# Strassen operand sums made by the producer and spilled, and one plain pair per stage

## The chip, the cores and the metric

The kernel runs on one core of one Trainium2 chip. The metric is the time of one execution in microseconds (us) on the device. Engines are named as in the profile: PE (TensorE), DVE (VectorE), ACT (ScalarE), POOL (GpSimd) and SP (SyncE); SP computes nothing and issues most transfers, and 16 DMA engines carry them.

## The reference

One decoder layer in float32, for 512 tokens of 2048 features. What matters here is the sequence of matrix products after the attention part:

```
merged = sigmoid(g_a) * (y_a @ w_up_a) + sigmoid(g_b) * (y_b @ w_up_b)
x  = x + merged @ w_o                                   # 2048 x 2048
h  = rmsnorm(x, ffn_norm_g)
hid = h @ w_ffn_in                                      # 2048 x 11264
x  = x + (silu(gate) * up) @ w_ffn_out                  # 5632 x 2048
x  = x + sigmoid(rmsnorm(x, ple_norm_g) @ w_ple_gate) * (p @ w_ple)
```

## The kernel before, in words

Activations are kept transposed: features on the 128 partitions, the 512 tokens along the row. A *unit* is 256 features of the contraction, so its operand is four blocks of 128 x 256 (two feature halves by two token halves), called b0 to b3. Every number is split into a high part (`hi`, made on ACT) and a low rest (`lo`, made on DVE), and a product takes high x high, high x low and low x high.

A *pair* (class `Pair`) computes 256 output features from all units of a stage (eight in most). A unit enters a pair in one of two kinds. Kind `P`, plain: eight block products, in twelve matmuls 512 wide (`mm3`, lines 286 to 298). Kind `S`, Strassen: seven products of sums of blocks. Its operand has seven blocks: the four plain ones, and three sums of them; the fourth plain block is overwritten by another sum (b3 − b1, held as `v`) once the plain form is no longer used. A pair of `S` alone issues 512- and 256-wide matmuls on line 694 (`doubled=7`); a pair with both kinds uses `mm3` 256 wide (the gate: `doubled=5`). `mix`, `mix_doubled` and `rest` recombine the products on DVE and ACT (lines 720, 750, 753, 799).

Weights come in *doubles* (two units). For `S` five blocks are landed from memory by SP (lines 341, 343), two more are added onto them by an accumulating transfer from POOL (line 363), and two sums are made on DVE (line 375); for `P` four blocks are landed (line 339). ACT splits the high part (line 359), DVE the low (line 356). Four landing buffers and three slots of split weights turn round.

The stages follow each other: the up-projections write the merged rows ("mix"), w_o makes x1, FFN-in (44 pairs) makes the inner rows ("hid", 22 units), FFN-out runs in three passes over 8, 8 and 6 units (`PASSES`), the last making x2, and the gate product closes. The rows of one stage are the units of the next. They are stored to memory (`spill`) and loaded again (`load`, line 518) as a *form* (`late_form`, `plain_first`): the first load is split to the plain blocks; a second load of the same row is gained and summed on DVE (line 527) into the three sums and `v`, which are then split. Until both are there a unit enters as `P`: the tuples `HALF`, `FFN_UNTIL`, `PLAIN_UNTIL`, `GATE_UNTIL` say for how many pairs each unit is plain.

What is loaded when is decided while the program is written out. `tick` runs after a part of each pair (eight times a pair of eight units): it fetches a first load for one of the next three forms, steps the first form, fetches one second load, and runs what was put off with `after`. A form whose plain use is over and whose second load has not been fetched is *urgent*: while there is one, no first load is fetched. Working blocks lie in the arena `wholes`, operands in `parts`, which has room for eight Strassen forms. Outputs of pairs, squares of rows and the like go to two 'out' buffers that turn round (`wide`). `Norm.add` squares a row (ACT) and adds it up (DVE).

Of the kernel before, what the change touches and what calls it, by code (L numbers as in the profile page):

```python
# [19 lines left out]
P = 128  # L20
# [35 lines left out]

PRODUCTS = (1, 2), (5, 4), (4, 3), (3, 6), (0, 5), (2, 0), (6, 1)

# [12 lines left out]
def hybrid_layer(  # L71
# [137 lines left out]
    def tick():  # L209
# [235 lines left out]
    class Form(Staged):  # L445


        def __init__(self, kind, steps, sizes, ready, src=None, far=False):
# [4 lines left out]
            self.second, self.due_second, self.forced, self.stage = None, 0, False, -1  # L453

        def fetch(self):
# [76 lines left out]
    def plain_first(form, raw, gain):  # L532
# [25 lines left out]
        if form.used:  # L558
            tt(b[:, 2:0:-1], b[:, 4:2:-1], twice(b[:, 1]))
            tt(b[:, 3], b[:, 2], b[:, 0], ALU.add)  # L560
            yield
            split_into(x[:, 3:7, 0], x[:, 3:7, 1], b[:, 1:5])
            give(w)
            return
        v = take(256, "old")
        tt(v.f(), b[:, 3], b[:, 1])
        tt(b[:, 2], b[:, 4], b[:, 1])
        tt(b[:, 3], b[:, 2], b[:, 0], ALU.add)
        yield
        split_into(x[:, 4:7, 0], x[:, 4:7, 1], b[:, 2:5])  # L570
        give(w)
        yield
        while not form.used:
# [4 lines left out]
    def all_first(form, raw):  # L578
# [4 lines left out]
        split_into(x[:, 0:4, 0], x[:, 0:4, 1], b)  # L583
        tt(t[:, 2], b[:, 3], b[:, 2])
        tt(v.f(), b[:, 3], b[:, 1])
        tt(t[:, 0], t[:, 2], b[:, 1])
        tt(t[:, 1], t[:, 0], b[:, 0], ALU.add)
        give(raw)
# [9 lines left out]

    def late_form(src, ready=always, gain=None, far=False):
# [10 lines left out]
        return Form("S", steps, [(parts, 2 * PLACE, "place"), (wholes, 1024, "low")], ready,  # L610
                    src, far)

# [336 lines left out]
    class Norm:  # L949
# [4 lines left out]
        def add(self, raw):  # L954
# [8 lines left out]
            if self.done == KU:  # L963
                self.chain = Staged(self.steps())
                self.chain.go_on()

        def steps(self):
# [309 lines left out]
    def plan_rest():  # L1277
# [5 lines left out]
        for j in range(KU):  # L1283
            plan(w_o[j], now("S" * KU, HALF, j))
        for m in range(KH):
# [16 lines left out]
    for n, ((w, i), pr) in enumerate(zip(order, made())):  # L1302
# [25 lines left out]
        else:  # L1328
# [9 lines left out]
             for j in range(KU)}  # L1338
    there = set()

    def spilled_form(kind, n, j, gain=None, **how):
        return (late_form if kind == "S" else plain_form)(
            lambda size=1024: load(spill[n, j], size), lambda: (n, j) in there, gain, far=True,
            **how)

# [7 lines left out]
    for j in range(KU):  # L1353
        for b in "ba":
# [13 lines left out]
            else:  # L1368
                nc.vector.tensor_tensor(out=g, in0=g, in1=part[j].f(), op=ALU.add)
# [13 lines left out]
    for j in range(KU):  # L1383
        h = load(xT[j])
        if j == 1:
            build(fs)
        pr = pair(ms, last=j == KU - 1, j=j, until=HALF, doubled=7)
        pr.onto(h.f())
        nc.sync.dma_start(out=spill["x1", j], in_=h.f())
        there.add(("x1", j))  # L1390
        norm2.add(h)
        give(h)
# [6 lines left out]
    for kinds in PASSES:  # L1399
        hs.append([spilled_form(k, "hid", u)  # L1400
                   for u, k in enumerate(kinds, sum(map(len, hs)))])
    def hidden(m, o):
        g, row2 = o[:, :T], norm2.row()
# [23 lines left out]
    for c, units in enumerate(hs):  # L1427
# [3 lines left out]
        for j in range(KU):  # L1431
# [14 lines left out]
            there.add(("x2", j))  # L1446
            norm3.add(h)
            give(h)
# [128 lines left out]
```

## Time and profile before

| | |
|---|---|
| median of 3 runs | 2655.95 us (2654.94 to 2663.76) |
| profiled execution, span | 2655.1 us |
| PE, DVE, ACT, POOL busy | 99%, 85%, 53%, 17% of the span |
| moved by DMA | 561.46 MB, mean 211 GB/s; 51.38 MB written to memory |
| granted PE clock | 0.999 |

The profiled execution's span is the time from its first to its last instruction, and the only time that the profile gives for it. A busy PE is not a PE at its best: matmuls overlap, so what a stage costs is read from the time between the starts of its pairs. "DMA share" in a window is the mean busy share of the 16 DMA engines; PE, DVE and the others stand with their busy time and, in brackets, their instructions.

### The profile page before, as it was taken

How to read it: one execution, taken by the hardware profiler on the slowest of the kernel's cores; microseconds unless marked ns; L12 is line 12 of the kernel's file. 1: busy time of each engine (PE TensorE's matmuls, PEld its weight loads, DVE VectorE, ACT ScalarE, POOL GpSimd, SP SyncE). 2: the span in 40 equal slices, each digit the busy share in tenths (PEclk: the TensorE clock that was granted, in tenths of full speed). 3: DMA queues.
4: the chain of work that ended last, by engine and by line, in shares of the span. 5: the costliest groups of instructions: out<-in, count | busy, mean ns of one | idle time of the engine just before them, and what ended most of it. 6: DMA issues, size and time to landing. Idle time of an engine off the chain costs nothing.

```text
span 2655.1 us, 42310 instructions
## 1 busy us (share of the span) xinstructions
PE 2633.3 (99%) x15188; PEld 2299.5 (87%) x15188; DVE 2254.2 (85%) x3856; ACT 1410.3 (53%) x2245; POOL 449.9 (17%) x556
## 2 busy tenths in 40 slices
PE   8999999999999999999999999999999999999998
PEld 6888888888998888888888888888888888889888
DVE  8687878787887558999888888888889989989897
ACT  7756565655554334566444444444445545455643
POOL 0122223232220001101111111111110211211010
PEclk9999999999999999999999999999999999999999
DMA  7676777777775668978888888888787989988784
GB/s 228 161 197 168 192 174 186 177 187 184 181 187 190 230 209 269 265 236 212 229 215 215 199 201 210 197 205 200 196 214 218 259 221 276 230 233 262 241 274 132
DMA packets 288130, 561.46 MB, mean 211 GB/s; under 512 B 26288, under 2 KB 133552, under 8 KB 287920
## 3 DMA queue, kind: packets, MB, share of 16 engines
q1 hardware_dynamic: 226576, 442.87, 50.9%
q0 software_dynamic: 61344, 115.89, 27.5%
q8 instruction: 119, 1.95, 0.3%
q14 instruction: 91, 0.75, 0.1%
HBM read 507.28 MB, written 51.38 MB: 210 GB/s over the span
## 4 chain that ended last, share of the span: by engine, by line
PE 94%; DVE 3%; ACT 1%; DMA 1%; issue 1%; SPq 0%; POOL 0%; ACTq 0%; DVEq 0%
PE ps L694 56%; PE ps L298 9%; PE ps L297 9%; PE ps L296 9%; PE small L694 6%; DVE wlo L356 1%; PE small L1158 1%; PE small L1106 1%; PE small L1032 1%; DVE wholes L527 0%; DVE parts L287 0%; DVE wholes L375 0%; ACT whi L359 0%; PE small L1217 0%; PE small L298 0%
## 5 line engine op out<-in xcount | busy, mean ns | idle before, releaser
L694 PE MATMUL ps<-parts,whi 128*128 128x512 f32 x4390 | 1470.1, 398 | 1.7 <-DVE out L799 1.3
L359 ACT ACTIVATE whi<-wholes 128x512 fp32r<-128x512 f32 (+2 forms) x934 | 874.3, 948 | 757.8 <-DVE wholes L375 295.3
L356 DVE TENSOR_TENSOR wlo<-wholes,whi 128x512 fp32r<-128x512 f32 (+2 forms) x934 | 982.5, 1087 | 79.5 <-ACT whi L359 78.7
L694 PEld LDWEIGHTS ps<-parts,wlo 128*128 128x128 f32 x4390 | 824.2, 188 | 187.3 <-issue 1.9
L694 PE MATMUL ps<-parts,wlo 128*128 128x256 f32 x4390 | 868.2, 279 | 0.9 <-DVE wlo L356 0.9
L694 PEld LDWEIGHTS ps<-parts,whi 128*128 128x128 f32 x4390 | 706.8, 189 | 10.3 <-issue 3.1
L296 PE MATMUL ps<-parts,whi 128*128 128x256 f32 (+1 forms) x1612 | 534.0, 333 | 6.9 <-ACT parts L286 4.9
L298 PE MATMUL ps<-parts,wlo 128*128 128x256 f32 (+1 forms) x1622 | 539.3, 333 | 0.7 <-DVE wlo L356 0.6
L297 PE MATMUL ps<-parts,whi 128*128 128x256 f32 (+1 forms) x1622 | 539.3, 333 | 0.7 <-DVE parts L287 0.5
L375 DVE TENSOR_TENSOR wholes<-wholes 128x256 f32<-128x256 f32 x820 | 347.0, 423 | 17.7 <-DVE wlo L356 2.8
L753 DVE TENSOR_TENSOR out<-out,ps 128x256 f32<-128x256 f32 x525 | 217.4, 417 | 158.0 <-ACT out L750 157.8
L297 PEld LDWEIGHTS ps<-parts,whi 128*128 128x128 f32 x1622 | 306.3, 189 | 37.6 <-DVE parts L287 2.6
L296 PEld LDWEIGHTS ps<-parts,whi 128*128 128x128 f32 x1612 | 304.0, 189 | 38.4 <-ACT parts L286 5.9
L298 PEld LDWEIGHTS ps<-parts,wlo 128*128 128x128 f32 x1622 | 306.7, 189 | 30.8 <-DVE wlo L356 2.0
L363 POOL DMA_DIRECT2D wholes<-w_ffn_in x169 | 147.1, 870 | 702.5 <-DMA wholes<-w_ffn_in 205.8
L363 POOL DMA_DIRECT2D wholes<-w_in x132 | 117.1, 888 | 527.5 <-DVE wholes L375 111.3
L694 PE MATMUL small<-parts,whi 128*128 128x512 f32 x480 | 190.2, 397 | 0.0
L287 DVE TENSOR_TENSOR parts<-wholes,parts 128x1024 fp32r<-128x1024 f32 (+3 forms) x139 | 124.5, 906 | 17.7 <-ACT parts L286 17.7
L750 ACT ACTIVATE out<-ps 128x256 f32<-128x256 f32 x279 | 105.1, 385 | 61.4 <-PE ps L694 56.9
L286 ACT ACTIVATE parts<-wholes 128x1024 fp32r<-128x1024 f32 (+3 forms) x139 | 107.9, 797 | 54.4 <-DVE wholes L527 37.7
L363 POOL DMA_DIRECT2D wholes<-w_ffn_out x64 | 55.7, 871 | 358.1 <-DVE out L753 76.7
L1405 ACT ACTIVATE out<-out 128x512 f32<-128x512 f32 x44 | 27.8, 633 | 152.2 <-DVE out L1404 152.2
(132 smaller groups left out, 1825.3 us busy)
## 6 DMA issues: line engine op xcount, KB each, us to landing
wholes<-w_ffn_in SPq DMA_DIRECT2D x169, 384.0 KB, 5.6
wholes<-w_in SPq DMA_DIRECT2D x132, 384.0 KB, 5.0
wholes<-w_ffn_in SPq DMA_DIRECT2D x169, 256.0 KB, 4.8
wholes<-w_ffn_in POOLq DMA_DIRECT2D x169, 256.0 KB, 5.4
wholes<-w_in SPq DMA_DIRECT2D x132, 256.0 KB, 4.0
wholes<-w_in POOLq DMA_DIRECT2D x132, 256.0 KB, 5.1
wholes<-w_ffn_out SPq DMA_DIRECT2D x64, 384.0 KB, 6.0
wholes<-x SPq DMA_DIRECT2D x46, 512.0 KB, 6.0
```

Of the source, the lines that this page charges most:

```text
L286: return (nc.scalar.activation(hi, src, AF.Copy), nc.vector.tensor_tensor(out=lo, in0=src, in1=hi.bitcast(F32), op=ALU.subtract))
L287: nc.vector.tensor_tensor(out=lo, in0=src, in1=hi.bitcast(F32), op=ALU.subtract))
L296: nc.tensor.matmul(ps, sh, mh, start=start, stop=False)
L297: nc.tensor.matmul(ps, sh, ml, start=False, stop=False)
L298: return nc.tensor.matmul(ps, sl, mh, start=False, stop=stop)
L356: in_turn(nc.vector.tensor_tensor(out=self.lo[:, blocks], in0=r, in1=h.bitcast(F32), op=ALU.subtract))
L359: in_turn(nc.scalar.activation(h, r, AF.Copy))
L363: nc.gpsimd.dma_start(out=raw[:, 3:5], in_=self.src[:, 1:3], accum_op=ALU.add)
L375: in_turn(nc.vector.tensor_tensor(out=o, in0=x, in1=y, op=ALU.add))
L694: m = nc.tensor.matmul(out, l, r, start=first and k == 0, stop=last and k == 1)
L750: in_turn(nc.scalar.activation(out, x, AF.Copy, scale=scale))
L753: in_turn(nc.vector.tensor_tensor(out=out, in0=x, in1=y, op=op))
```

## The change

The sums of a row are made where the row is made, and stored beside it: for the merged rows (`leave`), x1 and those x2 rows that the gate uses as Strassen units (`gained_sums`, after the gain), and the FFN inner rows (`hidden`, from the two halves of a unit that lie in the two 'out' buffers). The second load of a form now fetches the three sums and `v` as two blocks, and only splits them. It waits until the sums have been issued (`ready_second`). Every unit is plain in the first pair of its stage only. The products are renumbered to the order in which the sums lie.

```diff
-HALF = 1, 1, 1, 1, 2, 2, 2, 2
-PLAIN_UNTIL = HALF, HALF, (2, 2, 2, 2, 1, 1)
+O_UNTIL = (1,) * 8
+PLAIN_UNTIL = (1,) * 8, (1,) * 8, (1,) * 6
-GATE_UNTIL = 1, 1, 2, 2, 2, 2, 1, 1
+GATE_UNTIL = (1,) * 8
-FFN_UNTIL = 1, 1, 2, 2, 2, 2, 2, 2
+FFN_UNTIL = (1,) * 8
...
-PRODUCTS = (1, 2), (5, 4), (4, 3), (3, 6), (0, 5), (2, 0), (6, 1)
+PRODUCTS = (1, 2), (5, 5), (4, 3), (3, 4), (0, 6), (2, 0), (6, 1)
...
-            if (f.used or not any(b.stage == f.stage and b.ready() and not b.there
-                                  for b in builds)) and fits([(wholes, 5 * 256, "old")]):
+            if f.ready_second() and (
+                    f.used or not any(b.stage == f.stage and b.ready() and not b.there
+                                      for b in builds)) and fits(
+                        [(wholes, 768, "old"), (wholes, 256, "old")]):
                 f.fetch_second()
...
-            self.second, self.due_second = self.src(5 * 256), clock[0] + WAIT
+            self.second, self.due_second = self.sums(), clock[0] + WAIT
...
-        w = form.second
-        b = cut(w.f())
-        if gain:
-            gained(w.f(0, 1024), w.f(0, 1024), *gain)
-            yield
-        tt(b[:, 4], b[:, 3], b[:, 2])
...
-        v = take(256, "old")
-        tt(v.f(), b[:, 3], b[:, 1])
-        tt(b[:, 2], b[:, 4], b[:, 1])
-        tt(b[:, 3], b[:, 2], b[:, 0], ALU.add)
-        yield
-        split_into(x[:, 4:7, 0], x[:, 4:7, 1], b[:, 2:5])
-        give(w)
-        yield
+        t, v = form.second
+        split_into(x[:, 4:7, 0], x[:, 4:7, 1], cut(t.f()))
+        give(t)
         while not form.used:
             yield
         split_into(x[:, 3, 0], x[:, 3, 1], v.f())
...
+    def second_blocks(n, j):
+        blocks = take(768, "old"), take(256, "old")
+        d = sum_spill[n, j]
+        nc.sync.dma_start(out=blocks[0].f(), in_=d[:, 256:1024])
+        nc.sync.dma_start(out=blocks[1].f(), in_=d[:, 0:256])
+        return blocks
...
+    def sums_into(o, x):
+        tt(o[:, 0:2], twice(x[:, 3]), x[:, 1:3])
+        tt(o[:, 2], o[:, 1], x[:, 1])
+        tt(o[:, 3], o[:, 2], x[:, 0], ALU.add)
+
+    def spill_sums(n, j, o, x):
+        sums_into(cut(o), cut(x))
+        nc.sync.dma_start(out=sum_spill[n, j], in_=o)
+        there.add((n, j, "sums"))
+
+    def gained_sums(n, j, h, gi, sq):
+        t = wide()
+        gained(t, h.f(), gi, j)
+        return lambda: spill_sums(n, j, sq, t)
...
-                give(part.pop(j))
-                after(1, lambda j=j, s=s: store("mix", j, s))
+                def leave(j=j, s=s, other=other):
+                    spill_sums("mix", j, other.f(), s.f())
+                    give(other)
+                    store("mix", j, s)
+
+                after(1, leave)
...
-        norm2.add(h)
+        after(1, gained_sums("x1", j, h, g_ffn, norm2.add(h)))
...
+        halves.append(cut(o))
         if m % 2 == 1:
             there.add(("hid", m // 2))
+            (x, y), u = halves, m // 2
+            halves.clear()
+            if ("hid", u) in sum_spill:
+                tt(y[:, 2], y[:, 1], x[:, 1])
+                tt(y[:, 3], y[:, 1], y[:, 0])
+                tt(x[:, 2], y[:, 3], x[:, 1])
+                tt(x[:, 3], x[:, 2], x[:, 0], ALU.add)
+                for i, b in enumerate((y, x)):
+                    nc.sync.dma_start(out=cut(sum_spill["hid", u])[:, 2 * i : 2 * i + 2],
+                                      in_=b[:, 2:4])
+                there.add(("hid", u, "sums"))
...
-            norm3.add(h)
+            sq = norm3.add(h)
+            if GATE[j] == "S":
+                after(1, gained_sums("x2", j, h, g_ple, sq))
```

More of the change, by code (lines that the diff above doesn't have):

```diff
@@ L445, in hybrid_layer, with __init__ @@
     class Form(Staged):
-        def __init__(self, kind, steps, sizes, ready, src=None, far=False):
+        def __init__(self, kind, steps, sizes, ready, src=None, far=False, sums=None,
+                     ready_second=None):
             super().__init__(steps(self))
@@ L453, in __init__ @@
             self.second, self.due_second, self.forced, self.stage = None, 0, False, -1
+            self.sums, self.ready_second = sums, ready_second
         def fetch(self):
@@ L597, in all_first, with late_form @@
         give(v)
-    def late_form(src, ready=always, gain=None, far=False):
+    def late_form(src, ready=always, gain=None, far=False, sums=None, ready_second=None):
         def steps(form):
@@ L610, in late_form @@
         return Form("S", steps, [(parts, 2 * PLACE, "place"), (wholes, 1024, "low")], ready,
-                    src, far)
+                    src, far, sums, ready_second)
     def plain_form(src, ready=always, gain=None, raw=1024, how="low", far=False):
@@ L965, in add @@
                 self.chain.go_on()
+            return sq
         def steps(self):
@@ L1283, in plan_rest @@
         for j in range(KU):
-            plan(w_o[j], now("S" * KU, HALF, j))
+            plan(w_o[j], now("S" * KU, O_UNTIL, j))
         for m in range(KH):
@@ L1368, in hybrid_layer @@
             else:
-                nc.vector.tensor_tensor(out=g, in0=g, in1=part[j].f(), op=ALU.add)
-                give(part.pop(j))
-                after(1, lambda j=j, s=s: store("mix", j, s))
+                other = part.pop(j)
+                nc.vector.tensor_tensor(out=g, in0=g, in1=other.f(), op=ALU.add)
+                def leave(j=j, s=s, other=other):
[3 more added lines that the diff above has]
+                after(1, leave)
         if not j:
@@ L1386, in hybrid_layer @@
             build(fs)
-        pr = pair(ms, last=j == KU - 1, j=j, until=HALF, doubled=7)
+        pr = pair(ms, last=j == KU - 1, j=j, until=O_UNTIL, doubled=7)
         pr.onto(h.f())
@@ L1401, in hybrid_layer @@
                    for u, k in enumerate(kinds, sum(map(len, hs)))])
+    halves = []
     def hidden(m, o):
```

22 lines of the change are left out of this document (9 added, 13 removed).

## The prediction

> **What bounds the kernel now.** I read the page first (busy shares, chain, DMA queues), then the PE timeline for the places where the operations change form (line 694 is a Strassen pair, lines 296 to 298 a plain or mixed one), then windows cut at those places, then the waits and the chain in the windows that ran long.
>
> ```profile
> span 2655.1 us, 42310 instructions
> PE 2633.3 (99%) x15188; PEld 2299.5 (87%) x15188; DVE 2254.2 (85%) x3856; ACT 1410.3 (53%) x2245; POOL 449.9 (17%) x556
> q1 hardware_dynamic: 226576, 442.87, 50.9%
> q0 software_dynamic: 61344, 115.89, 27.5%
> PE 94%; DVE 3%; ACT 1%; DMA 1%; issue 1%; SPq 0%; POOL 0%; ACTq 0%; DVEq 0%
> ```
>
> TensorE is never off for long, so time is gained by issuing fewer columns or by closing the few holes. The sum is made against this execution's 2655.1 us, 0.03% under the median of 2655.95 us. A difference under about 0.3%, 8 us, can hardly be told from no change here.
>
> ```profile
> core 0: us, PE busy (x) PEld busy (x) DVE busy (x) ACT busy (x) POOL busy (x), PEclk, DMA share, GB/s
> 839.20:1005.10 165.90, 165.90 (x734) 137.41 (x733) 90.72 (x98) 58.28 (x65) 0.88 (x1) 1.00 0.64 216
> 1005.10:1068.80 63.70, 62.55 (x342) 53.95 (x341) 55.96 (x94) 33.52 (x44) 7.91 (x9) 1.00 0.92 276
> 1068.80:1146.90 78.10, 78.10 (x449) 68.15 (x448) 73.53 (x129) 38.83 (x52) 14.08 (x16) 1.00 0.93 253
> 1146.90:1166.70 19.80, 19.80 (x114) 17.21 (x113) 19.67 (x35) 13.17 (x20) 0.89 (x1) 1.00 0.68 208
> 1166.70:1231.70 65.00, 64.85 (x341) 55.38 (x340) 61.79 (x114) 47.08 (x70) 8.19 (x9) 1.00 0.82 237
> 1270.80:1973.70 702.90, 702.90 (x4033) 613.29 (x4032) 622.77 (x1117) 337.17 (x468) 126.14 (x145) 1.00 0.82 206
> 2032.50:2094.90 62.40, 62.40 (x343) 54.24 (x342) 61.85 (x103) 34.38 (x45) 8.77 (x10) 1.00 0.96 276
> 2192.70:2257.20 64.50, 63.12 (x343) 53.78 (x342) 61.42 (x100) 34.87 (x45) 9.64 (x11) 1.00 0.97 274
> 2355.10:2387.20 32.10, 32.10 (x146) 26.68 (x145) 29.24 (x49) 14.41 (x20) 4.38 (x5) 1.00 0.86 248
> 2387.20:2465.00 77.80, 77.80 (x546) 73.09 (x546) 71.92 (x111) 40.74 (x53) 6.97 (x8) 1.00 0.85 260
> 2481.10:2527.40 46.30, 45.49 (x219) 37.65 (x218) 41.14 (x71) 31.29 (x47) 4.72 (x5) 1.00 0.84 257
> 2527.40:2588.90 61.50, 61.50 (x365) 54.30 (x364) 55.35 (x89) 27.42 (x38) 7.92 (x9) 1.00 0.89 272
> ```
>
> The rows are, in order: the plain up-projections from the second on; w_o pairs 0 to 2; 3 to 6; 7; FFN-in pairs 0 to 2; 36 steady FFN-in pairs; the first three pairs of FFN-out pass 0; of pass 1; the first two of pass 2; pass 2's pairs 2 to 6; gate pairs 0 and 1; gate pairs 2 to 4. The reader should see three things. TensorE is full everywhere. VectorE is at 95 to 99% of the windows in which operands are made (61.79 of 65.00, 61.85 of 62.40, 61.42 of 64.50). And the DMA engines are at 0.92 to 0.97 there.
>
> **The price of a unit on TensorE.** The plain window holds 14 half-pairs of four units and five small products of the same twelve matmuls: 61 units, 2.72 us each. A Strassen unit costs 702.90 / 36 / 8 = 2.44 us in a pure pair, (77.80 / 5 − 2 x 2.72) / 4 = 2.53 in pass 2's mixed pair, and (61.50 / 3 − 2 x 2.72) / 6 = 2.51 in the gate's.
>
> **What the plain pairs become.** The second pair of each stage turns Strassen: 4 units in w_o, 6 in FFN-in, 4 in each of three passes, 4 in the gate, 26 together; pure pairs also lift the units that were mixed from 2.53 to 2.44. A plain pair takes 21.76, a pure one 19.53.
> - w_o: now 63.70, with 62.3 by the prices (21.76 + 4 x 2.53 + 4 x 2.72 + 19.53). After 21.76 + 2 x 19.53 = 60.8: gain 2.9 if the 1.4 us of holes go too.
> - FFN-in: now 65.0, by the prices 62.7; the other 2.3, the norm's small products and what they wait for, I keep. 60.8 + 2.3 = 63.1: gain 1.9.
> - Pass 0: 62.4 to 60.8, gain 1.6. Pass 1: 64.5 to 60.8, gain 3.7, of it 2.2 holes.
> - Pass 2: 32.1 to 16.3 + 15.6 = 31.9, gain 0.2, since its mixed pair is little cheaper than a plain one.
> - Gate: 4 x (2.72 − 2.51) = 0.8.
>
> Sum 11.1 us, 7.5 without the holes of w_o and pass 1.
>
> **Do the holes go?** They are VectorE's.
>
> ```profile
> PE ps L694 <- DVE out L799: 1.2, 2, 0.8
> PE ps L694 <- DVE wlo L356: 0.9, 1, 0.9
> by line: DVE wlo L356 22.6%; DVE wholes L527 22.5%; PE ps L694 22.1%; issue 12.2%; DVE parts L287 8.4%; DVE wholes L375 7.3%; DVE out L720 3.6%; PE ps L298 0.5%; PE ps L297 0.5%; PE ps L296 0.5%
> ```
>
> The first is w_o's start, the second pass 1's, the third the chain from 2225 to 2250 us: line 527, the consumer's sums, stands in front of the weight splits. Where those sums lie today:
>
> ```profile
> 1005.10:1068.80 63.70, 9.00 (x23) 1.00 0.92 276
> 1166.70:1231.70 65.00, 12.46 (x30) 1.00 0.82 237
> 2032.50:2094.90 62.40, 12.08 (x28) 1.00 0.96 276
> 2192.70:2257.20 64.50, 12.03 (x28) 1.00 0.97 274
> 2387.20:2465.00 77.80, 3.03 (x8) 1.00 0.85 260
> 2481.10:2527.40 46.30, 6.14 (x16) 1.00 0.84 257
> ```
>
> (VectorE's time on line 527 alone.) The change takes it away there and puts it where the rows are made.
>
> **What VectorE pays instead.**
>
> ```profile
> L356 DVE TENSOR_TENSOR wlo<-wholes,whi 128x1280 fp32r<-128x1280 f32 x8 | 11.9, 1487 | 0.1
> L375 DVE TENSOR_TENSOR wholes<-wholes 128x256 f32<-128x256 f32 x16 | 6.7, 421 | 0.1
> L356 DVE TENSOR_TENSOR wlo<-wholes,whi 128x512 fp32r<-128x512 f32 x8 | 5.5, 686 | 0.0
> L356 DVE TENSOR_TENSOR wlo<-wholes,whi 128x1024 fp32r<-128x1024 f32 x4 | 4.9, 1221 | 0.0
> ```
>
> A double of Strassen weights costs (11.9 + 6.7 + 5.5) / 8 = 3.0 us, a plain one 1.2: +1.8. A spilled sum is one 512-wide and two 256-wide instructions, 0.69 + 0.84 = 1.5 us; a unit of FFN inner rows four 256-wide, 1.7 per two pairs. A pure pair's recombination is 12 x 0.42 + 0.69 = 5.7 against a mixed one's 4 x 0.42 + 2 x 0.69 = 3.1: +2.6.
> - Up-projections: 1.5 per pair of half-pairs, and VectorE is at 90.72 of 165.90. Nothing; TensorE covers it. Steady FFN-in: 622.77 / 36 = 17.3 per pair plus 0.85, of 19.53. Nothing, with 1.4 us to spare.
> - w_o and the start of FFN-in as one stretch (1005.1 to 1231.7, 226.6 us): VectorE has 210.95. Out: 9.00 + 12.46. In: nine sums (the last merged row, eight x1) 13.8, one inner unit 1.7, five doubles 9.0, two recombinations 5.2. That is 219.2 of an ideal 221.8; in w_o pairs 3 to 7 alone it is 93.2 + 7.7 = 100.9 of 97.9, over by 3.0, of which weights split ahead and operands split late absorb part.
> - Pass 0: 61.85 − 12.1 + 3.6 + 2.6 = 56.0 of 60.8; pass 1 much the same. VectorE stops being tight. Pass 2's pairs 2 to 6: 71.92 − 3.0 + 5 x 1.5 = 76.5 of 77.8; between nothing and 2, I take 0.5. Gate: 41.1 − 6.1 + 3.6, easier.
>
> ScalarE does the gains it did before, at another time, and is at 53%. GpSimd gets 13 more accumulating transfers, at 17%: nothing.
>
> **What the DMA engines pay.** From the queue rows: 1.60 us of all 16 engines for 512 KB (442.87 MB in 50.9% of the span), 0.83 us for 128 KB accumulated (115.89 MB in 27.5%). A converted unit lands five blocks instead of four and accumulates two: 0.20 + 0.83 = 1.03. Sums are 42 stores of 512 KB, 22 MB; loads of them replace loads as large.
>
> ```profile
> 2094.90:2114.40 19.50, 19.50 (x114) 17.01 (x113) 17.45 (x32) 7.67 (x11) 5.83 (x7) 1.00 1.02 250
> ```
>
> - w_o and FFN-in's start: 58.6 + 72.6 + 13.5 + 53.3 = 198.0 now. Plus ten units 10.3, nine stores 14.4, one inner unit 1.6: 224.3, against 221.8 of TensorE. The fullest pair I found, above, has 1.02, so this stretch cannot reach its ideal: 2.5 back, and with VectorE's 3.0 in the same pairs I take 3.0, between 0 (transfers moved forward into the up-projections, share 0.64) and 7 (the two added, and late operands).
> - Pass 0: 59.9 + 4.1 = 64.0 of 60.8. The last FFN-in pair before it can take some, as the sums lie ready long before; I take 0.5 back, 0 to 3. Pass 1: 62.6 + 4.1 = 66.7 of 60.8; I take 1.5, 0 to 5.
> - Pass 2 and gate: 27.6 + 4.1 of 31.9; 38.9 + 4.1 of 45.5. Nothing.
>
> **Waits and queues.** SyncE waits in order, and a store of sums waits for VectorE:
>
> ```profile
> SPq L341 <- DVE wlo L356: 1331.1, 379, 10.1
> SPq L1389 <- DVE wholes L375: 26.5, 6, 5.4
> ```
>
> Behind a store stand the weight loads of line 341, which already wait 3.5 us each for the same engine to free a landing. The x1 store waits 4.4 us today; the second store behind it adds about the sums' 1.5, inside the weights' lead. SyncE issues 62 more stores and 42 more loads: nothing. The 'out' buffers of a pair are held one tick, an inner row's one pair longer, and are next written in the last quarter of the pair after: nothing. Were that cover gone, it would be one store's landing, some 5 us, per pair.
>
> **Sum.** 11.1 − 3.0 − 0.5 − 1.5 − 0.5 = 5.6: 2649.5, rounded to 2650.
>
> **Rivals.**
> (a) The DMA engines do not bind; their share only tells that work is queued. Then only VectorE's half microseconds are given back: 10 us gained, 2645. For it: pass 0 ran with 0.96 and no hole. Against it: pass 1 with 0.97 had holes, but VectorE's. [...] The trace does not decide it: its starts never moved more than 276.
> (b) The operands come late: second pairs now need all eight sums after one pair, not two, and each of five starts loses about 2 us. The gain is spent: 2655. For it: pass 1 still summed on line 527 in its third pair, from 2235.9 us on (first row below). Against it: VectorE, which delayed them, has less to do.
>
> ```profile
> 2240.73 0.42 DVE wholes L527
> wholes<-x SPq DMA_DIRECT2D x46, 512.0 KB, 6.0
> L286 ACT ACTIVATE parts<-wholes 128x1024 fp32r<-128x1024 f32 x8 | 8.3, 1052 | 2.6 <-DVE wholes L527 2.6
> L287 DVE TENSOR_TENSOR parts<-wholes,parts 128x1024 fp32r<-128x1024 f32 x9 | 11.0, 1220 | 0.0
> ```
>
> (c) Slower: used forms go first. While a used form has not loaded its second part, no first part is fetched, and from the third tick of a first pair all forms become used two at a time. If the last first half is not fetched in the first two ticks, TensorE meets a load and its split: landing 6.0 us, split 1.05 and 1.22 (rows above), about 8 us. It decides if two or more starts are hit: three give 24 − 5.6, some 2669, two 2660, centre 2664. Against it: seven of eight rows exist a pair earlier.
>
> **Chances.** Forecast 0.45 (2647 to 2654), (a) 0.25 (2643 to 2648), (b) 0.15 (2653 to 2660), (c) 0.15 (2659 to 2670). Range 2643 to 2663, leaving out the upper half of (c) and a little of (a). Faster than 2648: (a) and the forecast's lower edge, 0.30. Slower than 2664: 0.13 from (c) and the edge of (b). Within: 0.57.
>
> **What would show it.** Second pairs of w_o, FFN-in and passes 0 and 1 without lines 296 to 298 and near 19.5 us; line 527 gone; no wait of PE on line 799 or 356 at pass 1's start; w_o pairs 3 to 6 above 78.1 us with VectorE near full and DMA share near 1; written bytes up by 22 MB. A PE wait of several us on lines 286 or 287 in a first pair is (c); w_o pairs 3 to 6 still at 78.1 with a share over 1.0 is (a). I am wrong most if the list that places transfers orders them otherwise than the ticks do.

## The result, and the profile after

The changed kernel took 2671.41 us in the median of 4 runs (2667.22 to 2673.83), the kernel before 2655.9 beside it: 1.0054 times as long, interval 1.004 to 1.0068. That is 0.54% slower, where 2650 had been predicted and 2663 was the range's end. The profiled execution of the changed kernel was its fastest, 2667.22 us with a span of 2665.4, so its trace shows 10.3 us of the loss and not the whole of it. The page, busy times and bytes:

```profile
PE 2633.5 (99%) x15175; PEld 2299.6 (86%) x15175; DVE 2279.7 (86%) x3929; ACT 1418.5 (53%) x2277; POOL 455.7 (17%) x569
HBM read 512.39 MB, written 73.40 MB: 220 GB/s over the span
```

Written bytes rose by the predicted 22.0 MB, and TensorE's busy time is that of before: what its plain units saved came back as time. The stages, in the windows of the prediction (in order: w_o pairs 0 to 2; 3 to 6; FFN-in 0 to 2; three pairs of pass 0; of pass 1; pass 2 pairs 0 and 1; 2 to 6; gate pairs 0 and 1):

```profile
core 0: us, PE busy (x) PEld busy (x) DVE busy (x) ACT busy (x) POOL busy (x), PEclk, DMA share, GB/s
1004.00:1067.70 63.70, 61.23 (x322) 51.81 (x321) 56.73 (x94) 36.00 (x52) 8.78 (x10) 1.00 0.99 302
1067.70:1146.30 78.60, 78.38 (x450) 68.07 (x449) 76.74 (x139) 42.73 (x61) 14.99 (x17) 1.00 0.99 282
1166.00:1232.30 66.30, 64.58 (x338) 54.80 (x337) 63.61 (x113) 42.75 (x65) 10.81 (x12) 0.97 0.93 273
2033.20:2094.60 61.40, 60.86 (x321) 51.94 (x320) 57.71 (x93) 34.84 (x52) 11.34 (x13) 1.00 1.01 297
2192.40:2253.00 60.60, 60.60 (x321) 51.97 (x321) 55.34 (x88) 34.54 (x51) 11.37 (x13) 1.00 1.04 304
2352.50:2387.90 35.40, 33.39 (x183) 29.39 (x182) 30.10 (x47) 19.86 (x28) 3.52 (x4) 0.95 0.91 254
2387.90:2472.40 84.50, 80.88 (x548) 74.96 (x546) 72.40 (x110) 40.58 (x53) 7.84 (x9) 0.98 0.87 260
2489.40:2538.10 48.70, 45.64 (x234) 38.79 (x233) 40.61 (x66) 26.40 (x39) 6.44 (x7) 0.96 0.94 297
```

Against before, first column: w_o's start 0, FFN-in's +1.3, pass 0 −1.0, pass 1 −3.9, pass 2 +3.3 and +6.7, the gate +2.4. The rest of pass 1 gives another +1.6 and pass 2's last pair +0.9. So the loss is pass 2's, 10.9 us, and what was gained elsewhere is nearly spent at the other starts. (This trace is a favourable one up to pass 2: the ten traces of the same instructions took 65.7 us in w_o's start on the mean, as the experiments show.) Two things are to be seen in the row of pass 2's pairs 2 to 6: VectorE did 72.40 us of work where it had done 71.92, so it was not overloaded; and the granted clock is under 1, as in all four windows that lost over 1 us. Pairs 1, 3 and 4 of pass 2, each of which took 15.5 to 15.8 before:

```profile
2368.70:2387.90 19.20, 17.27 (x112) 16.13 (x111) 16.45 (x27) 11.72 (x18) 1.73 (x2) 0.91 0.83 247
2403.50:2423.40 19.90, 17.23 (x111) 16.09 (x110) 15.04 (x23) 8.96 (x13) 1.73 (x2) 0.91 0.86 270
2423.40:2439.50 16.10, 15.86 (x112) 14.72 (x110) 14.05 (x23) 7.45 (x10) 1.74 (x2) 1.00 0.90 278
```

What TensorE waited for from 2352 to 2520 us (us in all, times, longest; the kernel before had no such wait in pass 2 up to the gate):

```profile
PE ps L300 <- DVE wlo L358: 4.0, 5, 2.7
PE small L957 <- DVE wholes L946: 3.1, 1, 3.1
PE ps L299 <- DVE parts L289: 1.9, 1, 1.9
```

In this kernel's lines, 358 splits weights, 289 an operand, 531 makes the producer's sums, 942 and 946 square a row and add it up, 703 (ACT) and 706 (DVE) begin a pair's recombination, 1476 makes an x2 row.

**The small waits, every pair.** Here is the turn of one x2 row in the fifth pair, VectorE's timeline and then ScalarE's (start, us, what, and in brackets idle time and what ended it; the row, line 1476, was done at 2433.91):

```profile
2435.03 1.42 DVE L946 TENSOR_TENSOR wholes<-wholes,out 128x512 f32<-128x512 f32 x2 [1.13 <-ACT out L942]
2436.37 0.69 DVE L531 TENSOR_TENSOR out<-out 128x512 f32<-128x512 f32 x1
2437.09 0.88 DVE L531 TENSOR_TENSOR out<-out,out 128x256 f32<-128x256 f32 x2
2438.72 0.42 DVE L706 TENSOR_TENSOR out<-out 128x256 f32<-128x256 f32 x1 [0.75 <-ACT out L703]
2439.07 2.08 DVE L358 TENSOR_TENSOR wlo<-wholes,whi 128x1280 fp32r<-128x1280 f32 x2
```

```profile
2433.94 1.06 ACT L942 ACTIVATE out<-wholes 128x1024 f32<-128x1024 f32 x1 [3.88 <-DVE wholes L1476]
2434.91 1.32 ACT L526 ACTIVATE out<-wholes,gcol 128x512 f32<-128x512 f32 x2
2438.09 0.60 ACT L703 ACTIVATE out<-ps 128x512 f32<-128x512 f32 x1 [1.86 <-DVE out L531]
```

And the kernel before at the same place of a pair, ScalarE and then VectorE (its line 717 is the line 703 above, 527 the consumer's sums, 356 the weight split; the row, line 1444, was done at 2413.24):

```profile
2413.27 1.06 ACT L956 ACTIVATE out<-wholes 128x1024 f32<-128x1024 f32 x1 [2.63 <-DVE wholes L1444]
2414.24 0.58 ACT L717 ACTIVATE out<-ps 128x512 f32<-128x512 f32 x1
```

```profile
2413.15 1.55 DVE L527 TENSOR_TENSOR wholes<-wholes 128x256 f32<-128x256 f32 x4
2416.16 2.08 DVE L356 TENSOR_TENSOR wlo<-wholes,whi 128x1280 fp32r<-128x1280 f32 x2
```

Before, ScalarE squares the row and goes straight on to copy the pair's first product. After, it also gains the row into an 'out' buffer (line 526), VectorE sums from it, and only then may the first product go into that same buffer. ScalarE stands 1.86 us, VectorE behind it 0.75 us, and behind VectorE's line 706 in its queue is the weight split for which TensorE waits. From the row's end to that split 5.16 us pass here, where 2.92 passed before. Both times VectorE makes a row's sums in between. But the consumer's sums filled the time in which ScalarE squared the row, while the producer's need ScalarE's gain, so VectorE stands 1.13 us for the square and 0.75 us for the copy. Those 1.88 us are most of the 2.24 between the two. In pass 2, ScalarE waits like this in four pairs:

```profile
ACT out L703 <- DVE out L531: 7.5, 4, 1.9
```

**The large hole of pair 3** is another one. Its chain of waits:

```profile
2395.95 6.05 DMA x<-wholes
2402.01 5.65 DMA wholes<-x
2407.68 0.73 ACT parts L545
...
2409.52 1.41 DVE wlo L358
2410.98 0.58 PE ps L300
```

An x2 row is stored, loaded again for the gate and split, and the weight split comes behind that split on VectorE, which had nothing else to do for 3.68 us. Before, the same two stood the other way round (line 356 splits weights, 542 the gate's operand):

```profile
2405.95 0.69 DVE L356 TENSOR_TENSOR wlo<-wholes,whi 128x512 fp32r<-128x512 f32 x1 [1.49 <-ACT whi L359]
2406.56 1.41 DVE L542 SCALAR_TENSOR_TENSOR parts<-wholes,gcol,parts 128x512 fp32r<-128x512 f32 x2
```

### The profile page after: what moved, and what is told of

It is laid out like the page before. It is cut to its first block, busy times and chain, and to the rows that moved or that the text cites. A ratio compares the mean times of both kernels' runs of the same rounds, so it can differ in the third digit from the quotient of the medians.

```text
span 2665.4 us, 42624 instructions
## 1 busy us (share of the span) xinstructions
PE 2633.5 (99%) x15175; PEld 2299.6 (86%) x15175; DVE 2279.7 (86%) x3929; ACT 1418.5 (53%) x2277; POOL 455.7 (17%) x569
## 4 chain that ended last, share of the span: by engine, by line
PE 86%; DVE 7%; DMA 4%; issue 2%; ACT 1%; POOL 0%; SPq 0%; ACTq 0%; DVEq 0%; POOLq 0%
PE ps L680 54%; PE ps L300 8%; PE ps L299 7%; PE ps L298 7%; PE small L680 6%; DVE wlo L358 2%; DVE out L739 1%; DMA wholes<-w_ffn_out 1%; DMA wholes<-w_o 1%; DMA wholes<-x 1%; PE small L1093 1%; DVE wholes L377 1%; PE small L1145 1%; PE small L1019 1%; DVE parts L289 1%
## 5 line engine op out<-in xcount | busy, mean ns | idle before, releaser
L680 PE MATMUL ps<-parts,whi 128*128 128x512 f32 x4602 | 1541.2, 398 | 4.4 <-DVE wholes L794 1.7
L358 DVE TENSOR_TENSOR wlo<-wholes,whi 128x512 fp32r<-128x512 f32 (+2 forms) x947 | 994.5, 1084 | 85.9 <-ACT whi L361 85.4
L680 PE MATMUL ps<-parts,wlo 128*128 128x256 f32 x4602 | 910.9, 279 | 0.0
L680 PEld LDWEIGHTS ps<-parts,whi 128*128 128x128 f32 x4602 | 741.9, 189 | 14.8 <-issue 2.9
L298 PE MATMUL ps<-parts,whi 128*128 128x256 f32 (+1 forms) x1457 | 483.1, 333 | 7.6 <-ACT parts L288 4.9
L299 PE MATMUL ps<-parts,whi 128*128 128x256 f32 (+1 forms) x1464 | 486.9, 333 | 3.2 <-DVE parts L289 3.2
L300 PE MATMUL ps<-parts,wlo 128*128 128x256 f32 (+1 forms) x1464 | 485.4, 334 | 4.1 <-DVE wlo L358 4.1
L299 PEld LDWEIGHTS ps<-parts,whi 128*128 128x128 f32 x1464 | 279.0, 191 | 36.6 <-DVE parts L289 4.6
L298 PEld LDWEIGHTS ps<-parts,whi 128*128 128x128 f32 x1457 | 277.7, 191 | 35.5 <-ACT parts L288 5.8
L680 PE MATMUL small<-parts,whi 128*128 128x512 f32 x512 | 202.6, 396 | 0.0
L289 DVE TENSOR_TENSOR parts<-wholes,parts 128x256 fp32r<-128x256 f32 (+3 forms) x150 | 125.0, 849 | 15.0 <-ACT parts L288 14.9
L288 ACT ACTIVATE parts<-wholes 128x768 fp32r<-128x768 f32 (+3 forms) x150 | 107.6, 751 | 40.0 <-DMA wholes<-hid 14.8
L365 POOL DMA_DIRECT2D wholes<-w_ffn_out x70 | 61.1, 873 | 354.1 <-DMA wholes<-w_ffn_out 91.2
L680 PEld LDWEIGHTS small<-parts,wlo 128*128 128x128 f32 x512 | 96.4, 188 | 20.2
```

Source lines behind the costliest of these rows:

```text
L288: return (nc.scalar.activation(hi, src, AF.Copy), nc.vector.tensor_tensor(out=lo, in0=src, in1=hi.bitcast(F32), op=ALU.subtract))
L289: nc.vector.tensor_tensor(out=lo, in0=src, in1=hi.bitcast(F32), op=ALU.subtract))
L298: nc.tensor.matmul(ps, sh, mh, start=start, stop=False)
L299: nc.tensor.matmul(ps, sh, ml, start=False, stop=False)
L300: return nc.tensor.matmul(ps, sl, mh, start=False, stop=stop)
L358: in_turn(nc.vector.tensor_tensor(out=self.lo[:, blocks], in0=r, in1=h.bitcast(F32), op=ALU.subtract))
```

## Experiments

Stage times below are between the sixth matmuls of pairs, in each kernel's trace. All edits are to the changed kernel; `SUMS` names the rows whose sums their producer makes, and rows not named are summed by their consumer as before. Every ratio is to the kernel before, on the same chip.

**How far one trace can be read.** Many of the kernels below are edited late only, and issue the same instructions in the same order on every engine until then: the changed kernel, the first three below, the four on the x2 sums and no_urgent up to 2340 us, norm_fill up to FFN-in. So their traces repeat those stages. w_o's first pair took 22.7 to 28.3 us in these ten, its second 19.5 to 21.7, and w_o's start 63.7 to 67.5, 65.7 on the mean; the 63.7 of after is the lowest. Without norm_fill, the starts of passes 0 and 1 took 60.6 to 61.9 and 60.6 to 61.1, and pass 2 was reached at 2355.4 us on the mean, against 2355.1 in the one trace of before. As far as these traces tell, the change is a draw up to pass 2, and a reading of a few us in w_o from a single trace shows nothing.

**Which part loses.** Four kernels split the change by stage.

```diff
+SUMS = "mix", "x1", "hid"                     # no_x2_sums, no_x2_pass2_plain
-PLAIN_UNTIL = (1,) * 8, (1,) * 8, (1,) * 6
+PLAIN_UNTIL = (1,) * 8, (1,) * 8, (2, 2, 2, 2, 1, 1)   # pass2_plain, no_x2_pass2_plain
+SUMS = "x2",                                  # only_x2_sums, all plain counts as before
```

> The changed kernel, but the gate's units make their sums as before: a second load of the x2 row is summed by its consumer, and the last FFN-out pass neither makes nor stores sums. Everything else stays as changed, the one plain pair per stage too. Theory: the loss lies in FFN-out pass 2, where the x2 sums stand in VectorE's in-order queue between the recombination and the weight split of the next pair; pairs 3 to 7 of that pass were 8.0 us longer than before (89.9 against 77.9 + 4.1 at the old prices). Without the sums some 7 us come back and the time is 2661 to 2665. Rival, transfers: the 22 MB of stored sums fill the DMA engines everywhere; only 3 of the 22 go here, so at most 2 us come back, 2669 to 2671.

> The changed kernel with the second pair of FFN-out pass 2 plain again (its four Strassen units plain for two pairs as before). Theory: that pair was 19.2 us, and a plain one is 16.3, so 3 us come back: 2668 to 2669. Rival, that the lateness is handed on and the third pair waits instead: no change, 2671.

> Both together: no x2 sums, and the second pair of pass 2 plain. Theory: the two add, 10 to 11 us come back, 2659 to 2662 by the median of the changed kernel, and what stays above before is the start of FFN-in and of the gate. Rival, transfers: 2666 to 2669.

> The kernel before (all counts of plain pairs as before, sums of merged rows, x1 and inner rows made by the consumer), with the x2 sums alone made and stored in pass 2. Theory: pass 2 loses here too, from pair 2 on, 5 to 9 us: 2661 to 2665. Rival, that pass 2 suffers from the second plain pair alone or from the transfers as a whole: 2655 to 2657.

| kernel | median us | ratio | pass 2 pairs 0, 1 | pairs 2 to 7 |
|---|---|---|---|---|
| before | 2655.9 | | 32.1 | 94.0 |
| after | 2671.41 | 1.0054 [1.004, 1.0068] | 35.4 | 101.5 |
| no_x2_sums | 2662.81 | 1.002 [1.001, 1.0029] | 33.6 | 94.0 |
| pass2_plain | 2665.68 | 1.0033 [1.0021, 1.0044] | 32.1 | 101.7 |
| no_x2_pass2_plain | 2657.69 | 1.0006 [0.9997, 1.0016] | 32.1 | 94.0 |
| only_x2_sums | 2671.27 | 1.0054 [1.0039, 1.0069] | 32.1 | 99.6 |

Undoing the x2 sums takes back 8.6 us, undoing the one plain pair of pass 2 takes back 5.7, both 13.7: they nearly add up, and without them the change is a draw. The x2 sums put into the old kernel alone lose as much as the whole change, though not all of it in pass 2 (its FFN-in start took 69.8 us against 65.0, with no edit there). Most of that is spread between executions: hid_sums_only, below, issues the same instructions up to there, and came to the same late matmul of FFN-in's start in 61.1 us, where only_x2_sums took 64.0 and before 59.2.

**What of the x2 sums.** A producer's sums are three instructions on VectorE and a store. One kernel keeps the store and drops the sums, one keeps the sums and drops the store, one steps the gate's first forms two ticks later, one makes the sums on GpSimd.

```diff
-        sums_into(cut(o), cut(x))
+        if n != "x2": sums_into(cut(o), cut(x))                         # x2_store_no_sums
-        nc.sync.dma_start(out=sum_spill[n, j], in_=o)
+        if n != "x2": nc.sync.dma_start(out=sum_spill[n, j], in_=o)     # x2_sums_no_store
+    for f in gs: f.wait = 4      # x2_wait4: first step 4 ticks after the load
+    nc.gpsimd.tensor_tensor(...) # x2_pool: the four x2 sums, one by one
```

> The changed kernel without the three VectorE instructions that sum an x2 row; a block is still stored and loaded in their place (it holds the squares, so the gate's sums are left out of what is computed). Tells VectorE's work from the transfer. Theory 1, VectorE's in-order queue: pairs 4 to 7 of pass 2 fall from 66.0 us to near the 62.8 of before. Theory 2, transfers and SyncE's waits: they stay near 66.

> The changed kernel in which the x2 sums are made on VectorE but not stored; the gate's second load reads the plain x2 row instead (so its operands are not the sums). Theory 1, VectorE's queue: pairs 4 to 7 of pass 2 stay near 66 us. Theory 2, transfers and SyncE: they fall to near 62.8.

> The changed kernel in which a gate form is stepped four ticks after its first load is issued, not two, so that the split of a freshly stored x2 row enters VectorE's queue later. Theory: pair 3 of pass 2 was 19.9 us because that split stood in front of the next pair's weight split and its row had not landed; with the longer wait it falls to 16.5 or less, and the rest of the pass stays. Rival, that the pair waits for its own sums or stores: it stays near 20.

> The changed kernel with the x2 sums made on GpSimd instead of VectorE, four instructions 256 wide. Theory, VectorE's queue: pairs 4 to 7 of pass 2 fall from 66.0 to near 62.8 us, as they did when the sums were left out. Rival, that the sums' sources hold the pair's output buffers or that the two engines hinder each other: they stay above 65.

Pass 2's pairs 2 to 7 in the windows of x2_store_no_sums, x2_sums_no_store and x2_pool:

```profile
2391.40:2485.30 93.90, 93.90 (x656) 88.07 (x655) 83.50 (x121) 50.95 (x66) 7.92 (x10) 1.00 0.90 281
2388.90:2489.50 100.60, 96.84 (x656) 88.75 (x655) 89.31 (x134) 51.84 (x69) 7.87 (x9) 1.00 0.74 225
2393.50:2503.70 110.20, 100.47 (x656) 92.80 (x655) 83.25 (x123) 52.07 (x69) 22.59 (x29) 0.95 0.74 235
```

The store is innocent: with it and the higher DMA share of 0.90 the stretch takes 93.9. The sums alone cost 6.7 us for 5.8 us more of VectorE (89.31 − 83.50). VectorE's total is not the limit, since with GpSimd doing the sums it is down to 83.25 and the stretch is at its longest (in part by a granted clock of 0.95). What the two slow ones share is ScalarE's wait for the sums, longer where the summing engine is slower (x2_sums_no_store, then x2_pool, whose line 724 is the line 703 above; one of the 20 sum instructions took some 0.74 us on GpSimd, an estimate from POOL's 22.59 − 7.87 us in the last two rows, where VectorE took 0.42 for one of that shape in after):

```profile
ACT out L724 <- DVE out L532: 9.3, 5, 1.9
ACT out L724 <- POOL out L1382: 18.7, 5, 5.4
```

x2_store_no_sums has no such wait at all. In x2_pool VectorE makes none of these sums and still stands, with the split behind it (line 967 is the 946 above, 727 the 706; the row was done at 2461.90):

```profile
2463.03 1.42 DVE L967 TENSOR_TENSOR wholes<-wholes,out 128x512 f32<-128x512 f32 x2 [1.13 <-ACT out L963]
2468.08 0.42 DVE L727 TENSOR_TENSOR out<-out 128x256 f32<-128x256 f32 x1 [3.64 <-ACT out L724]
2468.43 2.09 DVE L358 TENSOR_TENSOR wlo<-wholes,whi 128x1280 fp32r<-128x1280 f32 x2
```

So the handing back of the 'out' buffer is enough to delay the split. The length of a pair goes with the time from the row's end to the split: at 2.6 to 3.3 us (once 3.7) a pair takes 15.6 us, at 5.2 some 16.5 (after's last three with sums), at 6.5 some 17.7 (x2_pool's last two, clock 1.00). With VectorE making the sums, the buffer is the smaller part. x2_store_no_sums has 3.33 us there, 0.44 of them the wait for ScalarE's copy; of the 1.83 us up to 5.16 the sums themselves are 1.5 and the longer wait 0.3. A third 'out' buffer could then return at most the 0.75 us of the wait; it was not tried, nor were the sums put behind the split in VectorE's queue.

The times: x2_store_no_sums 2662.06, 1.0017 [1.0006, 1.0027]; x2_sums_no_store 2667.78, 1.0041 [1.0024, 1.0058]; x2_pool 2680.59, 1.0096 [1.0078, 1.0115]. x2_wait4 gave 2667.47, 1.0041 [1.0025, 1.0057]: pair 3 fell from 19.93 to 15.84, as the chain above says, but pairs 4 and 5 rose to 17.32 and 16.95, and the stretch still took 99.2. The early load explained one pair, not the stretch.

**The starts of the other stages.** These ask why w_o's and FFN-in's starts gained nothing. All but hid_sums_only, norm_fill and the two mix_hid kernels have the x2 sums and pass 2's count undone, so 2657.69 is what they are to beat. In w_o's second pair, TensorE waited in after's trace for a buffer of the other kind, a PSUM bank: a pair of Strassen units alone uses all six large banks, and the plain pair before it holds two until its result is added (line 794):

```profile
PE ps L680 <- DVE wholes L794: 1.7, 1, 1.7
```

```diff
+narrow = name == small or (self.ends_small and name in ("y", "z"))
+self.banks[name] = small_bank() if narrow else bank()    # ends_small, small_no_urgent
-        for f in list(builds)[: 0 if urgent else AHEAD]:
+        for f in list(builds)[:AHEAD]:                   # no_urgent, small_no_urgent
```

> The kernel without x2 sums and with pass 2's second pair plain (median 2657.7), in which the first, plain pair of w_o and of passes 0 and 1 puts its two results into the two small PSUM banks. Theory: a pure Strassen pair takes six of the six large banks, so after a plain pair it waits until that pair's two large banks are read out (the 1.7 us hole on the x1 addition in w_o's second pair); with them elsewhere w_o's second pair falls from 21.5 to about 19.6 and the time by 2 to 3 us. Rival, that VectorE is simply late there: the hole stays, on another line.

> The same base (2657.7), but first loads are fetched also while a used form lacks its second part. Theory of my prediction's rival (c): the holes on lines 288 and 289 in w_o's first pair (0.7 and 0.8 us here, 2.8 in a sister kernel) are first halves held back by that rule; they go, and the time falls by 1 to 3 us. Rival, that those halves are late by their rows: no change, 2657 to 2658.

> Both on the same base. If both theories hold the gains add: 2652 to 2654, under before. If neither does, 2657 to 2658.

In ends_small's trace that pair took 20.15 us against 21.49 after, but that the bank made it shorter is not shown. small_no_urgent issues the same instructions, took 23.1 us there and waited for a bank all the same:

```profile
PE small L703 <- DVE wholes L817: 1.8, 1, 1.8
```

And five traces of the unedited instructions took 19.5 to 19.8 there, with no such wait. ends_small's first pair, 25.68 us against 22.67 after and 21.22 before, lies inside the spread as well.

The times were ends_small 2656.6, 1.0001 [0.9991, 1.0012]; no_urgent 2658.02, 1.0004 [0.9993, 1.0015]; small_no_urgent 2658.04, 1.0006 [0.9996, 1.0017]. The edit of no_urgent left the instructions of the program as they were: no_urgent issues those of no_x2_pass2_plain in the same order, small_no_urgent those of ends_small, and mix_hid_no_urgent, below, those of mix_hid. So urgent second halves never held back a first half in these kernels, and the mechanism of the prediction's rival (c) did not occur. These runs are repeats, and each pair of medians agrees within 1.5 us.

```diff
-                    spill_sums("mix", j, other.f(), s.f())
-                    give(other)
-                    store("mix", j, s)
+                    nc.sync.dma_start(out=spill["mix", j], in_=s.f())   # row_first
+                    there.add(("mix", j))
+                    spill_sums("mix", j, other.f(), s.f())
+                    give(other, s)       # late_give, late_give_small: after(4, ...)
```

> The base without x2 sums and with pass 2's second pair plain (2657.7), in which a merged row is stored first and its sums are made and stored after it, not before. Theory: the last merged row reached w_o's first pair late because its store stood on SyncE behind the store of its sums, which waits for VectorE; with the row first the holes on the operand splits in that pair go and it falls from 23.5 to between 21.2 and 22, the time by 2 us, to 2655 or 2656. Rival, that the DMA engines are full there: the holes stay.

> The base without x2 sums and with pass 2's second pair plain, merged row stored first, and the blocks of a merged row and of its sums given back four ticks later. Theory: the loads no longer wait in SyncE for the landing of two stores, the last operand of w_o comes some 5 us earlier, and w_o's first pair falls from 23.5 to 25 us to under 22; the time by 2 us, to 2655. Rival, that the row load waits for its own row's store alone or that the DMA engines are full: the hole of 2 us on the operand split stays.

> The same with the plain pair's results in the small PSUM banks. Theory: w_o's start at about 61 us, 2.8 under before, passes 0 and 1 some 4 under, FFN-in and gate 1 to 2 over: 2651 to 2654, 0.1 to 0.2% faster than before. Rival, that what one start gains another loses: 2656 to 2658.

row_first was meant to have the last merged row back sooner. The chain before the hole of w_o's first pair in its trace:

```profile
1005.27 7.18 DMA mix<-wholes
1012.45 0.02 SPq L1352
...
1012.92 5.04 DMA mix<-wholes
...
1018.03 5.21 DMA wholes<-mix
1023.26 1.07 ACT parts L288
1024.35 1.22 DVE parts L289
```

A transfer for another row on SyncE (line 1352, a load of sums) waits in SyncE's queue for the block that the first store still reads; the sums' store, and then the row's load, come after it in order. Three landings in a row, 17.4 us, stand before two splits. That giving the block back later helps or harms w_o can't be told, as all three first pairs lie inside the spread: row_first 2656.75, 1.0007 [0.9997, 1.0016], first pair 24.98; late_give 2662.31, 1.0027 [1.0017, 1.0036], 23.73; late_give_small 2661.31, 1.002 [1.0011, 1.0029], 25.31. The last two lost time in pass 1, whose second pair took 25.1 and 24.2 us (19.51 after): in late_give TensorE waited 3.1 us there for ScalarE's copy of a product.

```diff
+SUMS = "hid",          # hid_sums_only; passes 0 and 1 alone have one plain pair
+SUMS = "mix", "hid"    # mix_hid: also row first, small banks; w_o too has one plain pair
+# mix_hid_no_urgent: mix_hid and the edit of no_urgent
```

> The kernel before with the inner rows' sums alone made and stored by the producer, and one plain pair in FFN-out passes 0 and 1 only; w_o, FFN-in, pass 2 and the gate keep their counts, and merged rows, x1 and x2 are summed by the consumer. Theory: steady FFN-in hides these sums, and passes 0 and 1 gain 1.0 and 2 to 4 us as in the changed kernel, so it is 3 to 5 us under before, 2652 to 2654. Rival, that the four-operation sums and 10 MB of stores cost FFN-in what the passes gain: 2656 or more.

> Merged rows' and inner rows' sums alone are made by the producer (row first, small banks for the plain pair), with one plain pair in w_o and passes 0 and 1; FFN-in, pass 2 and the gate as before, x1 and x2 summed by the consumer. Theory: w_o's start falls from 63.8 to 61, passes 0 and 1 keep their 3 to 4 us, the rest is as before: 2649 to 2652, faster than before by 0.2%. Rival, that each start's time depends on the order in which transfers happen to be placed: some other start loses what these gain, 2655 to 2660.

> The same, with first loads fetched also while a used form lacks its second part. Theory: takes away the hole on a first half in pass 0's first pair, if that comes back as it did with the inner rows' sums alone; 2649 to 2652. Rival: as the one above, 2655 to 2660.

hid_sums_only took 2666.97, 1.0038 [1.0024, 1.0052]; mix_hid 2661.63, 1.0022 [1.0014, 1.0031]; mix_hid_no_urgent 2661.29, 1.0018 [1.0009, 1.0027]. These keep passes 0 and 1, which had gained, and drop the x2 sums and pass 2's count, and still lose. In hid_sums_only the starts of passes 0 and 1 took 65.8 and 65.7 us, against 61.4 and 60.6 after, and mix_hid's pass 1 65.5; all three are well outside the spread of these stages. In hid_sums_only TensorE waited 2.9 us in pass 0 for ScalarE's part of an operand (line 288). The list that places transfers may order everything anew with each edit upstream, so that a stage's gain is not its own; that this is why these starts lost is my reading and is not shown.

**The norm's holes.** norm_fill puts small matmuls before the two norms' column sums (4 and 10), to see whether they keep TensorE's clock up.

```diff
+            for _ in range(self.fill):
+                nc.tensor.matmul(ps[:, :P], ones, ident, start=True, stop=True)
```

> The changed kernel with small matmuls of no use (ones by identity, 128 wide) put on TensorE in front of the norm's column sums: four for the norm after w_o, ten for the norm after pass 2, where TensorE had holes of 0.9 and 3.1 us and the granted clock then fell to 0.5 for 3.4 us. Theory, that the holes cost twice because of the clock: the drop after the second is gone, and gate pair 0 falls from 27.8 to about 26 us, the whole by 1 to 3 us, although TensorE does more. Rival, that the hole is the whole cost: gate pair 0 stays at 27.8 or rises, no change in time.

2672.38, 1.006 [1.0045, 1.0075]. At the gate the hole fell from 3.06 to 1.72 us, and FFN-in's first pair took 24.93 us against 26.01; the granted clock of the whole profiled execution was 0.998, against 0.997 after. No saving can be told, and the run does not settle what the clock needs.

## Why the prediction was wrong

- **The prices held.** The second pairs of w_o, FFN-in and passes 0 and 1 lost lines 298 to 300, and pass 1's start took 60.60 with 60.8 forecast as its bare price. Consumer sums are gone.
- **The step that failed** is "The 'out' buffers of a pair are held one tick, an inner row's one pair longer, and are next written in the last quarter of the pair after: nothing". In pass 2 the next pair's recombination begins earlier and takes the gained row's buffer, and the sums that hold it wait for ScalarE, where the consumer's had not. From a row's end to the weight split behind it in VectorE's queue, 5.2 us passed in place of 2.6 to 3.3, in every pair with such sums. With it failed the term of pass 2, "76.5 of 77.8; between nothing and 2, I take 0.5": measured 6.7 over the same pairs, 7.5 with the last. Of the 6.7, some 4.3 are pair 3's, where the gate's early load and the clock after it come in, which the sum did not have either; but x2_wait4 shortened that pair and the stretch with the last pair still lost 5.2. I took VectorE's total for its limit. The total came out at 72.40, less than the 76.5 I had summed, and the pairs were still late, since the split stood in VectorE's queue behind its waits (1.13 and 0.75 us in the fifth pair).
- **Pass 2's start** had gain 0.2 and lost 3.3. The one price I saw was TensorE's; second loads of the inner rows then had one pair less to land, and TensorE waited 1.9 us on line 289. That is rival (b), in one stage. Its "about 2 us" was the hole's size; the clock of 0.50 for 3.4 us after it cost some 1.7 more, by the estimate below.
- **The clock** was no term at all, as the trace of before kept 1.00 in every window shown. Four falls to 0.50 cost some 6.8 us of the trace's 10.3, by an estimate of 1.7 each (below).
- **w_o**, gain 2.9 with 3.0 given back, measured 0 in this trace. That is luck of one execution: ten traces of the same instructions took 65.7 us on the mean, a loss of 2.0. In nine of them TensorE waited 0.7 to 2.8 us in the first pair for ScalarE's part of a late operand (line 288); line 527 is gone. Why it was late is traced in row_first only, so the cause stays open. Pairs 3 to 6, named as the place where VectorE and the DMA engines run over, went from 78.1 to 78.6 here, and took 78.1 to 81.1 in the ten.
- **FFN-in** forecast −1.9, measured +1.3 (64.9 to 66.3 us in traces of the same instructions, 65.0 before): two waits round the norm, 0.9 and 0.8 us, and a fall of the clock. **The gate** forecast −0.8, measured +2.4: the norm's hole of 3.1 us (line 946) and a fall of the clock. I had counted VectorE's work at both and not what the norm's chain waits for.
- **Pass 0 and pass 1** forecast −1.1 and −2.2, measured −1.0 and −3.9, of which 1.6 comes back in pass 1's later pairs.
- **Rival (a)** was right on its ground. Pass 1's start ran without a hole at a DMA share of 1.04 and 304 GB/s, above the 276 of before, so a share near 1 was no bound there. Nor did VectorE's busy share show the limit in pass 2's pairs 2 to 6: 72.40 of 84.50 us were busy where VectorE's queue was what TensorE waited for.
- **Rival (c)**, 2659 to 2670, came nearest to 2671.41, by a mechanism that did not occur, so its nearness is luck. Its sum also takes the gain off twice: three starts of 8 us less 5.6 of gain give 2673.5, two 2665.5. And its upper half is 0.075 and (b) ends at 2660, which does not make the 0.13 put on slower than 2664.
- What stays open: why the same instructions take up to 5.6 us more or less in w_o's first pair, and what share of pass 2's loss a third 'out' buffer would return.

## What to carry to other kernels

Before moving work from a consumer to a producer, follow the buffer that the moved work reads: who writes it next, how soon, and which queue stands behind that writer. Ask also what the work now has to wait for, where before it filled a wait. VectorE, in order and 86% busy, set the pace here, so sum such an engine's waits with its work, and price the first late operand of a stretch at its hole plus the slow clock that may follow (in pass 2's start 1.9 us and some 1.7). Where a greedy list places the transfers, measure each part alone and together; parts that gained in company lost alone here. And find kernels whose instructions agree over a stretch: they show how far one profiled execution of it can be trusted, which here was 5.6 us in w_o's first pair.

## What the runs showed of the hardware

In the trace of after, up to its last 2 us, the granted clock fell to 0.50 four times, at 1178.7, 2373.3, 2410.9 and 2506.4 us, and each time for 3.4 us. TensorE had holes of 0.95 and 0.78 us there at the first, 1.93 at the second, 2.67 at the third and 3.06 at the fourth; the fall came within the last hole or up to 1.6 us after its end. After w_o's hole of 1.71 us, which ended at 1032.0, the clock stayed at 1.00. First the time after that hole, then the four falls:

```profile
1032.00:1035.40 3.40, 3.36 (x19) 2.99 (x20) 3.40 (x7) 2.78 (x4) 0.87 (x1) 1.00 1.01 370
1178.70:1182.10 3.40, 2.94 (x7) 2.37 (x8) 3.40 (x9) 1.34 (x3) 1.14 (x1) 0.50 1.08 302
2373.30:2376.70 3.40, 3.40 (x18) 3.40 (x18) 3.40 (x6) 1.11 (x1) 0.00 (x0) 0.50 0.59 106
2410.90:2414.30 3.40, 3.32 (x15) 3.33 (x16) 3.40 (x6) 2.30 (x3) 0.27 (x1) 0.50 0.79 205
2506.40:2509.80 3.40, 3.40 (x10) 2.62 (x9) 3.40 (x7) 1.78 (x3) 0.96 (x1) 0.51 0.74 279
```

The length of a hole alone does not tell whether the clock falls. In the trace of before, a hole of 2.18 us that ended at 641.7 (line 1217) was followed by 1.00 from there to 645.1 us, longer than the 1.93 us that a fall followed here. What decides it was not shown.

If TensorE's work goes with the clock, 3.4 us at 0.50 cost 1.7 us; that is an estimate. The matmuls of the third row give 1.5: those of 128x256 started 0.21 us apart in it, and 0.12 apart just before. With 1.7, pair 1 of pass 2 is 15.6 + 1.9 + 1.7 = 19.2 and pair 3 15.6 + 2.7 + 1.7 = 20.0, against 19.20 and 19.90 measured.
